# A hybrid encoder block on one core: closing steps of a head group ordered between weight pieces, and q, k, v projections in 512-column products

## The chip, the cores and the metric

The kernel runs on one core of one Trainium2 chip, in one launch. The metric is the device time of a run in microseconds (us). The engines are PE (TensorE: matmuls, and weight loads shown as PEld), DVE (VectorE), ACT (ScalarE), POOL (GpSimd) and SP, which issues the DMA transfers. Each engine works through its own instruction list in order; semaphores hold an instruction until what it needs is there.

## The reference

For one sequence of 256 tokens of width 2048:

```python
h = rms_norm(x, g_mix)
q, k, v, z, f, scal, gates = split(h @ w_in)      # 1024 x5, 32, 4096 columns
y_a = gated_deltanet_branch(q, k, v, z, scal, ...)   # conv, silu, l2 norm, 8 heads of 128,
                                                     # chunks of 64, forward and backward
y_f = real(fft2(f by groups of 128)) @ w_fourier
gate_a, gate_f = split(sigmoid(gates))
x = x + (gate_a * y_a + gate_f * y_f) @ w_o
x = x + square(relu(rms_norm(x, g_mlp) @ w_mlp_up)) @ w_mlp_down
return rms_norm(x, g_final)
```

In the DeltaNet branch each chunk of 64 tokens solves a unit lower triangular system, and chunks are linked by a state per head, in both directions.

## The kernel before

All weights stream once from memory, in pieces of 512 KB (128 x 1024 floats). SP issues the load into a tile `raw` (four buffers). `split` makes two tiles of it (three buffers each): `hi`, a rounded copy on ACT (L88), and `lo`, the remainder, by a subtraction on DVE (L92). The activations are split in the same way, side by side in one tile: `hh[:, k, 0]` is `h_hi`, `hh[:, k, 1]` is `h_lo`. PE sums `hi*hi + hi*lo + lo*hi`. So no weight piece reaches PE before DVE has made its `lo`.

In the order of the streams: k of the first four heads (9 pieces), the other five chunks of q, k, v (40 pieces of `w_qkv`), `w_in` (32 pieces, for z and f), the gates (`w_g`, 64 pieces, eight to a chunk of 512 columns; a gate piece is named here by its number, so the second chunk has pieces 9 to 16), among them and behind them the branches' outputs (`w_dn`, `w_fo`), then `w_o` and the MLP. Two ways of multiplying matter here.

- `pair_fm` (L104 to L130) makes two 128-column blocks of q, k or v, feature-major (features on the partitions), both in one PSUM bank of 512 columns. Per k (16 of them for each block) it issues three products of 256 columns (L121, L122, L127). DVE then multiplies both blocks from PSUM by `rbc`, the rms factor, into `u` (L321). Ten such pairs.
- `stream` (L156) multiplies the other way round: a weight piece of 2 k's by 512 columns is the moving side, and two PSUM banks (token halves) are filled. A gate piece is 12 products of 512 columns (L168 to L170).
- `tile_fm` (L131) exists for the MLP: per k one product of 512 columns (L146), whose moving side is `hi | lo` of the activations, and one of 256 (L149). The two halves of the bank are then added by `add_halves`: a copy on ACT (L153) and an addition on DVE (L154).

The DeltaNet branch works on two groups of four heads, gi = 0 and 1. For a group, DVE inverts small triangles by substitution in 16 steps (L489 `tf`, L491 `Xf`, on a layout made by a round trip through memory: `Mf`). `Xf` goes to memory (`dscr`, L493) and comes back in another layout (`Xh`, eight loads, L498), is copied into `Xc` by ACT (L500) and transposed in blocks by DVE and ACT into `De` and `DT` (L505 to L508). PE joins them into larger inverses (L521, L528, L540, L544). The closing steps of a group follow one from the other: L574 (state, `sF` on DVE L575), L580 (`rS` on DVE L582), L587 (copied by ACT, L588), L593 and L596 (outputs), L601, L604.

The order on every engine is not written by hand: a scheduler with a simulated timeline orders the program's instructions by its own costs and by dependencies. An explicit dependency without a semaphore can be added between two instructions of one engine; it only fixes which comes first.

Of the kernel before, what the change touches and what calls it, by code (L numbers as in the profile page):

```python
# [11 lines left out]
ALU = mybir.AluOpType  # L12
PSUM = bass.MemoryType.PSUM

P = 128
T = 256
# [11 lines left out]
def encoder_block_kernel(ctx, tc, xT, x, g_mix, w_qkv, w_k0, w_in, w_g, w_sc, conv_w, hprm, g_head, w_dn, w_fo, w_o,  # L28
# [16 lines left out]
    def mm_ps():  # L45
        return psm.tile([P, NW], F32, tag="mm", name=nm("mm"))
# [49 lines left out]
    def wtiles(a=KP, n=NW, parts=True):  # L96
        raw = st.tile([P, a, n], F32, tag="raw", bufs=4, name=nm("raw"))
        if not parts:
            return raw, None, None
        hi = st.tile([P, a, n], F32R, tag="hi", bufs=3, name=nm("hi"))  # L100
        lo = st.tile([P, a, n], F32R, tag="lo", bufs=3, name=nm("lo"))
        return raw, hi, lo

    def pair_fm(srcs, ahi, alo):  # L104

        nk = srcs[0].shape[1]
        ps = mm_ps()
        last = None
        for j, src in enumerate(srcs):
            o = ps[:, j * T:j * T + T]  # L110
            for q in range(nk // 8):
                raw, hi, lo = wtiles()
                nc.sync.dma_start(raw.rearrange("p a b -> p (a b)"),
                                  src.rearrange("p k n -> p (k n)")[:, q * 1024:q * 1024 + 1024])
                split(hi, lo, raw)
                hv = hi.rearrange("p a b -> p (a b)")
                lv = lo.rearrange("p a b -> p (a b)")
                for kk in range(8):
                    k = 8 * q + kk
                    cs = slice(kk * P, kk * P + P)  # L120
                    first = pe.matmul(o, hv[:, cs], ahi[:, k, :], start=(k == 0), stop=False)  # L121
                    pe.matmul(o, hv[:, cs], alo[:, k, :], start=False, stop=False)  # L122
                    if last is not None:
                        tc.add_manual_dep(first.ins, last.ins.name, mybir.DependencyInfo(
                            mybir.DependencyClass.NoSync, mybir.DependencyReason.DATA), reason="one group at a time")
                        last = None
                    end = pe.matmul(o, lv[:, cs], ahi[:, k, :], start=False, stop=(k == nk - 1))  # L127
            last = end
        return ps

    def tile_fm(src, ab):  # L131

        ps = mm_ps()
# [18 lines left out]
    def add_halves(dst, ps):  # L152
        act.copy(dst, ps[:, T:2 * T])  # L153
        dve.tensor_tensor(dst, ps[:, 0:T], dst, op=ALU.add)  # L154

    def stream(src, nk, ahi, alo):  # L156

        ps = [mm_ps(), mm_ps()]
        for k0 in range(0, nk, KP):
            raw, hi, lo = wtiles()  # L160
            nc.sync.dma_start(raw, src[:, k0:k0 + KP, :])
            split(hi, lo, raw)
            for kk in range(KP):
                k = k0 + kk
                for tb in range(2):
                    sl = slice(tb * P, tb * P + P)
                    ah, al = ahi[:, k, sl], alo[:, k, sl]
                    pe.matmul(ps[tb], ah, hi[:, kk, :], start=(k == 0), stop=False)  # L168
                    pe.matmul(ps[tb], ah, lo[:, kk, :], start=False, stop=False)  # L169
                    pe.matmul(ps[tb], al, hi[:, kk, :], start=False, stop=(k == nk - 1))  # L170
        return ps


# [133 lines left out]
    def qkv_chunk(c, ps=None):  # L307

        u = pd.tile([P, 4, T + 4], F32, tag="u", bufs=1, name=nm("u"))
        pool.memset(u[:, :, 0:2], 0.0)  # L310
        pool.memset(u[:, :, T + 2:T + 4], 0.0)
        y = pd.tile([P, 4, T], F32, tag="y", bufs=1, name=nm("y"))
        done = 0
        while done < 4:
            if ps is None:
                p = pair_fm([w_qkv[4 * c + done], w_qkv[4 * c + done + 1]], h_hi, h_lo)
                p = p.rearrange("p (a b) -> p a b", a=2)
            else:
                p = ps[done]
            n = p.shape[1]  # L320
            dve.tensor_tensor(u[:, done:done + n, 2:T + 2], p, rbc.unsqueeze(1).to_broadcast([P, n, T]), op=ALU.mult)  # L321
            for j in range(done, done + n):
                cb = 4 * c + j
                act.activation(y[:, j, :], u[:, j, 0:T], AF.Copy, scale=cw[:, cb, 0:1])
                for w in range(1, 5):
                    dve.scalar_tensor_tensor(y[:, j, :], u[:, j, w:w + T], cw[:, cb, w:w + 1], y[:, j, :],
                                             op0=ALU.mult, op1=ALU.add)
            done += n
        return y
# [230 lines left out]
    def dn_out(gi, Kt, offg, offk, rho, Pt, rq, ec):  # L560
        DTv = DT.rearrange("p (d t h) i -> p d t h i", d=2, t=2)
        Y = Kt if gi == 0 else pd.tile([P, 2, 2, 4, P], F32, tag="Kt", name=nm("Y"))
        ohat.append(pd.tile([P, 2, 4, P], F32, tag=f"ohat{gi}", name=nm("ohat")))
        sF = pd.tile([P, 2, 4, P], F32, tag="sF", name=nm("sF"))
        rS = pd.tile([P, 2, 4, P], F32, tag="rS", name=nm("rS"))
        tmp = pd.tile([P, 2, 4, P], F32, tag="tf", name=nm("tmp"))

        def heads_ps():
            return dn_ps().rearrange("p (a b) -> p a b", a=4)

        for d in range(2):
            py = heads_ps()
            for h in range(4):
                pe.matmul(py[:, h], DTv[:, d, d, h], rho[:, d, h], start=True, stop=True)  # L574
            dve.tensor_tensor(sF[:, d], py, ec[:, d].unsqueeze(2).to_broadcast([P, 4, P]), op=ALU.mult)  # L575
            act.copy(Y[:, d, d], py)
        for d in range(2):
            p1 = heads_ps()
            for h in range(4):
                pe.matmul(p1[:, h], offg[d][:, h], sF[:, d, h], start=True, stop=True)  # L580
            for h in range(4):
                dve.scalar_tensor_tensor(rS[:, d, h], p1[:, h], nea[:, 8 * d + 4 * gi + h:8 * d + 4 * gi + h + 1],  # L582
                                         rho[:, 1 - d, h], op0=ALU.mult, op1=ALU.add)
        for d in range(2):
            py = heads_ps()
            for h in range(4):
                pe.matmul(py[:, h], DTv[:, d, 1 - d, h], rS[:, d, h], start=True, stop=True)  # L587
            act.copy(Y[:, d, 1 - d], py)  # L588
        for tb in range(2):
            d = 1 - tb  # L590
            po = heads_ps()
            for h in range(4):
                i1 = pe.matmul(po[:, h], Pt[:, 0, tb, h], Y[:, 0, tb, h], start=True, stop=False)  # L593
                if h:
                    tc.keep_in_program_order(i1)
                i2 = pe.matmul(po[:, h], Pt[:, 1, tb, h], Y[:, 1, tb, h], start=False, stop=True)  # L596
                tc.keep_in_program_order(i2)
            act.activation(tmp[:, d], po, AF.Copy, scale=-1.0)
            p2 = heads_ps()
            for h in range(4):  # L600
                pe.matmul(p2[:, h], offk[:, 1 - tb, h], sF[:, d, h], start=True, stop=True)  # L601
            oh = ohat[gi][:, tb]
            for h in range(4):
                dve.scalar_tensor_tensor(oh[:, h], p2[:, h], eab[:, 8 * d + 4 * gi + h:8 * d + 4 * gi + h + 1],  # L604
                                         tmp[:, d, h], op0=ALU.mult, op1=ALU.add)

            ov = pd.tile([P, 4], F32, tag="ov", bufs=2, name=nm("ov"))
            for h in range(4):
                act.activation(tmp[:, d, h], oh[:, h], AF.Square, accum_out=ov[:, h:h + 1])
            rqt = rq[:, 4 * tb:4 * tb + 4]  # L610
            r2 = pd.tile([P, 4], F32, tag="r2", bufs=2, name=nm("r2"))
            pool.tensor_tensor(r2, rqt, rqt, op=ALU.mult)
            pool.tensor_tensor(ov, ov, r2, op=ALU.mult)
            pool.tensor_scalar(ov, ov, 1.0 / P, EPS, op0=ALU.mult, op1=ALU.add)
            pool.tensor_tensor(ov, ov, neg_half[:, 0:4], op=ALU.pow)
            pool.tensor_tensor(fsc[:, gi, tb], ov, rqt, op=ALU.mult)
# [34 lines left out]
    def gates(dst, c):  # L651

        ps = stream(w_g[c], KD, h_hi, h_lo)
        for tb in range(2):
            act.activation(dst[tb], ps[tb], AF.Tanh, scale=rstdh[:, tb:tb + 1])  # L655
# [3 lines left out]
    def m_cols(c):  # L659
        return [merged[:, tb, c * NW:c * NW + NW] for tb in range(2)]  # L660

    for c in range(4):
        gates(m_cols(c), c)


    o_hi = pd.tile([P, NH, T], F32R, tag="Kt", name="o_hi")
# [312 lines left out]
```

## Time and profile before

| | |
|---|---|
| median of 3 runs | 1390.75 us (1389.53 to 1393.6) |
| profiled execution | 1391.09 us, span 1389.3 us |
| mean granted clock of PE | 0.997 |
| PE busy | 1373.4 us (99%) |
| DVE busy | 864.2 us (62%) |
| ACT busy | 688.5 us (50%) |
| loads of weights | 250 MB of 255.6 MB, mean 184 GB/s |

A row of a group gives busy time and mean ns of one instruction, then the idle time of the engine before them and what ended it. A row of the timeline starts with the start in us and the duration. A matmul's duration includes its way through the array, so the pace of PE is read from starts, not from durations. Idle time of an engine that is not the bound costs nothing.

### The profile page before, as it was taken

Reading aid. Unit: us, or ns where it says so; the run is one execution under the profiler, and the core shown is the slowest. Engines: PE = TensorE matmul, PEld = TensorE weight load, DVE = VectorE, ACT = ScalarE, POOL = GpSimd, SP = SyncE. Lnnn points to the kernel's source line nnn. Section 1 sums busy time; section 2 is a strip of 40 time slices with the busy share of each in tenths; the row PEclk is TensorE's granted clock in tenths of the full one; section 3 lists DMA queues with packets and bytes.
Section 4 is the critical chain, followed back from the end, with each engine's and each line's share of the span. In section 5 each row is a group of like instructions: output and inputs, shape, how many; then the busy total and the mean of one; then the engine's idle time right before and its main releaser. Section 6 shows DMA issues by size and latency. Waiting matters only on the chain.

```text
span 1389.3 us, 19766 instructions
## 1 busy us (share of the span) xinstructions
PE 1373.4 (99%) x7646; PEld 1188.0 (86%) x7646; DVE 864.2 (62%) x1233; ACT 688.5 (50%) x1038; POOL 36.0 (3%) x60
## 2 busy tenths in 40 slices
PE   9999999999999999999999999999999999999997
PEld 8999997888888888888888888888888888888886
DVE  7869997855556555655666666444456666645553
ACT  6586746454444444455554454333345445434443
POOL 2001010100000000000000000000000000000000
PEclk9999999999999999999999999999999999999999
DMA  8456455354566556676565556666665555666663
GB/s 288 148 168 184 152 166 176 93 166 137 176 201 181 156 177 188 194 269 186 175 200 185 193 193 188 193 190 195 195 196 183 192 190 192 185 197 193 190 197 132
DMA packets 88399, 255.61 MB, mean 184 GB/s; under 512 B 25456, under 2 KB 25456, under 8 KB 87920
## 3 DMA queue, kind: packets, MB, share of 16 engines
q1 hardware_dynamic: 87312, 250.15, 58.8%
q10 hardware_dynamic: 992, 4.19, 0.8%
q8 instruction: 60, 0.98, 0.3%
q14 instruction: 35, 0.29, 0.1%
HBM read 251.16 MB, written 3.15 MB: 183 GB/s over the span
## 4 chain that ended last, share of the span: by engine, by line
PE 94%; issue 1%; DVE 1%; DMA 1%; ACT 1%; SPq 1%; POOLq 0%; POOL 0%; DVEq 0%; ACTq 0%
PE mm L146 17%; PE mm L170 10%; PE mm L169 10%; PE mm L168 10%; PE mm L149 9%; PE mm L831 7%; PE mm L829 7%; PE mm L830 7%; PE mm L122 3%; PE mm L121 3%; PE mm L127 3%; PE mm L866 1%; PE mm L864 1%; PE mm L865 1%; DVE lo L92 0%
## 5 line engine op out<-in xcount | busy, mean ns | idle before, releaser
L92 DVE TENSOR_TENSOR lo<-raw,hi 128x1024 fp32r<-128x1024 f32 (+1 forms) x459 | 560.8, 1222 | 339.4 <-ACT hi L88 330.7
L88 ACT ACTIVATE hi<-raw 128x1024 fp32r<-128x1024 f32 (+1 forms) x459 | 485.9, 1059 | 422.6 <-PE mm L831 181.7
L146 PE MATMUL mm<-hh,hi 128*128 128x512 f32 x1024 | 245.1, 391 | 0.0
L146 PEld LDWEIGHTS mm<-hh,hi 128*128 128x128 f32 x1024 | 188.2, 188 | 36.2
L831 PE MATMUL mm<-hi,rl 128*128 128x512 f32 x448 | 174.6, 390 | 0.0
L830 PE MATMUL mm<-lo,rh 128*128 128x512 f32 x448 | 174.5, 389 | 0.0
L829 PE MATMUL mm<-hi,rh 128*128 128x512 f32 x448 | 156.2, 390 | 0.0
L169 PE MATMUL mm<-lo,hh 128*128 128x512 f32 x384 | 151.4, 394 | 0.0
L170 PE MATMUL mm<-hi,hh 128*128 128x512 f32 x384 | 150.8, 393 | 0.0
L168 PE MATMUL mm<-hi,hh 128*128 128x512 f32 x384 | 142.4, 392 | 0.4 <-ACT merged L655 0.4
L149 PEld LDWEIGHTS mm<-hh,lo 128*128 128x128 f32 x1024 | 131.5, 191 | 5.1
L149 PE MATMUL mm<-hh,lo 128*128 128x256 f32 x1024 | 133.2, 283 | 0.0
L153 ACT COPY rt<-mm 128x256 f32<-128x256 f32 x64 | 23.8, 372 | 164.5 <-PE mm L146 164.5
L831 PEld LDWEIGHTS mm<-hi,rl 128*128 128x128 f32 x448 | 84.2, 188 | 17.5
L830 PEld LDWEIGHTS mm<-lo,rh 128*128 128x128 f32 x448 | 84.1, 188 | 17.5
L829 PEld LDWEIGHTS mm<-hi,rh 128*128 128x128 f32 x448 | 84.1, 188 | 17.3
L154 DVE TENSOR_TENSOR rt<-mm,rt 128x256 f32<-128x256 f32 x64 | 27.2, 424 | 110.5 <-ACT rt L153 110.5
L122 PE MATMUL mm<-hh,hi 128*128 128x256 f32 x320 | 90.8, 284 | 0.0
L121 PE MATMUL mm<-hh,hi 128*128 128x256 f32 x320 | 90.7, 284 | 0.0
L127 PE MATMUL mm<-hh,lo 128*128 128x256 f32 x320 | 90.5, 284 | 0.0
L168 PEld LDWEIGHTS mm<-hi,hh 128*128 128x128 f32 x384 | 71.9, 188 | 15.2 <-ACT merged L655 0.6
L169 PEld LDWEIGHTS mm<-lo,hh 128*128 128x128 f32 x384 | 72.5, 189 | 14.2
(309 smaller groups left out, 1690.4 us busy)
## 6 DMA issues: line engine op xcount, KB each, us to landing
raw<-in_w_up_dram SPq DMA_DIRECT2D x128, 512.0 KB, 3.9
raw<-in_w_down_dram SPq DMA_DIRECT2D x128, 512.0 KB, 3.5
raw<-in_w_g_dram SPq DMA_DIRECT2D x64, 512.0 KB, 3.8
raw<-in_w_qkv_dram SPq DMA_DIRECT2D x40, 512.0 KB, 4.2
raw<-in_w_in_dram SPq DMA_DIRECT2D x32, 512.0 KB, 3.9
raw<-in_w_o_dram SPq DMA_DIRECT2D x32, 512.0 KB, 4.4
raw<-in_w_dn_dram SPq DMA_DIRECT2D x16, 512.0 KB, 3.6
raw<-in_w_fo_dram SPq DMA_DIRECT2D x16, 512.0 KB, 3.6
```

The source lines that it names most:

```text
L88: act.activation(hi, src, AF.Copy, scale=scale)
L92: dve.tensor_tensor(lo, src2, hi.bitcast(F32), op=ALU.subtract)
L121: first = pe.matmul(o, hv[:, cs], ahi[:, k, :], start=(k == 0), stop=False)
L122: pe.matmul(o, hv[:, cs], alo[:, k, :], start=False, stop=False)
L146: pe.matmul(ps, hv[:, cs], ab[:, k].rearrange("p a b -> p (a b)"), start=(k == 0), stop=(k == KD - 1))
L149: pe.matmul(ps[:, 0:T], lv[:, cs], ab[:, k, 0], start=False, stop=False)
L168: pe.matmul(ps[tb], ah, hi[:, kk, :], start=(k == 0), stop=False)
L169: pe.matmul(ps[tb], ah, lo[:, kk, :], start=False, stop=False)
L170: pe.matmul(ps[tb], al, hi[:, kk, :], start=False, stop=(k == nk - 1))
L829: pe.matmul(ps[tb], ah, hi[:, kk, :], start=(k == 0), stop=False)
L830: pe.matmul(ps[tb], ah, lo[:, kk, :], start=False, stop=False)
L831: pe.matmul(ps[tb], al_, hi[:, kk, :], start=False, stop=(k == 31))
```

## The change

`pair_fm` is gone; each q, k, v block is a `tile_fm` in a bank of its own, followed by a copy on ACT and an addition on DVE, and for each pair of blocks one multiplication by `rbc` from SBUF. `stream` notes the last product of each piece in `ends`. The closing steps of group 0 note six first products in `steps` (two of L580, two of L587, two of L593). After the second gate chunk is written, `spread(0)` orders step i behind the last product of piece i of that chunk.

```diff
-    def pair_fm(srcs, ahi, alo):
...
+    ends = []
+    steps = []
+
+    def spread(s0):
+
+        for step, end in zip(steps[s0:], ends):
+            tc.add_manual_dep(step.ins, end.ins.name, mybir.DependencyInfo(
+                mybir.DependencyClass.NoSync, mybir.DependencyReason.DATA), reason="weights between the steps")
...
     def stream(src, nk, ahi, alo):
 
         ps = [mm_ps(), mm_ps()]
+        ends.clear()
...
-                    pe.matmul(ps[tb], al, hi[:, kk, :], start=False, stop=(k == nk - 1))
+                    end = pe.matmul(ps[tb], al, hi[:, kk, :], start=False, stop=(k == nk - 1))
+            ends.append(end)
...
-                p = pair_fm([w_qkv[4 * c + done], w_qkv[4 * c + done + 1]], h_hi, h_lo)
-                p = p.rearrange("p (a b) -> p a b", a=2)
+                n = 2
+                for j in range(done, done + n):
+                    p = tile_fm(w_qkv[4 * c + j], hh)
+                    uj = u[:, j, 2:T + 2]
+                    act.copy(uj, p[:, T:2 * T])
+                    dve.tensor_tensor(uj, p[:, 0:T], uj, op=ALU.add)
+                un = u[:, done:done + n, 2:T + 2]
+                dve.tensor_tensor(un, un, rbc.unsqueeze(1).to_broadcast([P, n, T]), op=ALU.mult)
...
-                pe.matmul(p1[:, h], offg[d][:, h], sF[:, d, h], start=True, stop=True)
+                i1 = pe.matmul(p1[:, h], offg[d][:, h], sF[:, d, h], start=True, stop=True)
+                if gi == 0 and h == 0:
+                    steps.append(i1)
...
     for c in range(4):
         gates(m_cols(c), c)
+        if c == 1:
+            spread(0)
```

The scheduler makes a new order from it. On PE, at the closing steps of group 0, before: the steps stand in one piece (numbers behind names tell tiles apart; `rho`, `sF`, `rS` are the chunk states of the group, `off` its link matrices).

```order
L170 MATMUL mm_3358<-hi_3486,hh 128x512
L574 MATMUL dn_1728<-rho_1214,DT 128x128 x4
L580 MATMUL dn_1735<-sF_1718,off_666 128x128 x4
L580 MATMUL dn_1744<-sF_1718,off_666 128x128 x4
L587 MATMUL dn_1753<-rS_1719,DT 128x128 x4
L587 MATMUL dn_1759<-rS_1719,DT 128x128 x4
L593 MATMUL dn_1765<-grp_528 128x128
```

After, on PE, the second of the L580 steps (now L571) and the first of the L587 steps (now L580), with `hi_3274` of gate piece 11 and `hi_3292` of piece 12:

```order
L571 MATMUL dn_1636<-sF_1610,off_666 128x128 x4
L151 MATMUL mm_3236<-hi_3274,hh 128x512
L152 MATMUL mm_3236<-lo_3275,hh 128x512
L153 MATMUL mm_3236<-hi_3274,hh 128x512
L151 MATMUL mm_3236<-hi_3274,hh 128x512
L152 MATMUL mm_3236<-lo_3275,hh 128x512
L153 MATMUL mm_3236<-hi_3274,hh 128x512
L151 MATMUL mm_3235<-hi_3292,hh 128x512
L151 MATMUL mm_3236<-hi_3292,hh 128x512
L580 MATMUL dn_1645<-rS_1611,DT 128x128 x4
L152 MATMUL mm_3235<-lo_3293,hh 128x512
```

The steps now have weight products of half a piece or more between them; pieces 9, 10 and 11 are used half by half around them.

On DVE, at the end of the second group's inverse, before (`lo_3563` and `lo_3581` are the remainders of gate pieces 12 and 13):

```order
L491 TENSOR_TENSOR Xf_2248<-Xf_2248,tf_2249 128x16
L646 SCALAR_TENSOR_TENSOR zs_3055<-tz_3202,zs_3055 128x512
L673 SCALAR_TENSOR_TENSOR ohat_1717<-ohat_1717,fsc,zs_1227 128x128 x4
L646 SCALAR_TENSOR_TENSOR zs_3055<-tz_3206,zs_3055 128x512
L555 TENSOR_TENSOR E_1825<-E_1825,aux_3229 128x4x128
L555 TENSOR_TENSOR E_1825<-E_1825,aux_3238 128x4x128
L92 TENSOR_TENSOR lo_3563<-raw_3561,hi_3562 128x1024
L92 TENSOR_TENSOR lo_3581<-raw_3579,hi_3580 128x1024
L505 STREAM_TRANSPOSE De<-Xc_2333 32x8x32
```

After, the same place on DVE (`lo_3293` is the remainder of gate piece 12):

```order
L480 TENSOR_TENSOR tf_2087<-Mf_2085,Xf_2086 128x16
L482 TENSOR_TENSOR Xf_2086<-Xf_2086,tf_2087 128x16
L643 SCALAR_TENSOR_TENSOR zs_2785<-tz_2932,zs_2785 128x512
L643 SCALAR_TENSOR_TENSOR zs_2785<-tz_2936,zs_2785 128x512
L496 STREAM_TRANSPOSE De<-Xc_2171 32x8x32 x4
L575 SCALAR_TENSOR_TENSOR rS_1611<-dn_1627,nea,rho_1160 128x128 x4
L92 TENSOR_TENSOR lo_3293<-raw_3291,hi_3292 128x1024
```

Between `Xf` and `De` stood two `lo`, two `E` and one `ohat`; now only the two `zs` stand there, and `lo` of piece 12 comes behind `De`. The `lo` of piece 11 stands thirty steps of the inverse ahead of these rows.

On DVE, behind the end of the first group's inverse (`De<-Xc_803` is the first group's) the rows are now:

```order
L482 TENSOR_TENSOR Xf_718<-Xf_718,tf_719 128x16
L92 TENSOR_TENSOR lo_2862<-raw_2860,hi_2861 128x1024
L92 TENSOR_TENSOR lo_2880<-raw_2878,hi_2879 128x1024
L409 TENSOR_TENSOR rho_2528<-aux_2529,nk_2017 128x512
L92 TENSOR_TENSOR lo_2898<-raw_2896,hi_2897 128x1024
L409 TENSOR_TENSOR rho_2528<-aux_2535,nk_2017 128x512
L317 SCALAR_TENSOR_TENSOR y_2544<-u_2541,cw,y_2544 128x256 x4
L496 STREAM_TRANSPOSE De<-Xc_803 32x8x32
```

Before, there were three `lo`, one `rho` and sixteen `y` (convolution taps, L326) between the same two.

On ACT, the rows ahead of `hi` of gate piece 12 are now:

```order
L642 ACTIVATE zs_2785<-mm_2787,rstd 128x512
L491 COPY Xc_2171<-Xh_2162 128x16x2x16
L497 COPY De<-Xc_2171 32x8x32 x4
L88 ACTIVATE hi_3292<-raw_3291 128x1024
L88 ACTIVATE hi_3310<-raw_3309 128x1024
```

Before, `hi` of pieces 12 and 13 stood ahead of the copy into `Xc`.

More of the change, by code (lines that the diff above doesn't have):

```diff
@@ L102, in wtiles @@
         return raw, hi, lo
-    def pair_fm(srcs, ahi, alo):
[L106 to L129, printed above, removed]
     def tile_fm(src, ab):
@@ L315, in qkv_chunk @@
             if ps is None:
-                p = pair_fm([w_qkv[4 * c + done], w_qkv[4 * c + done + 1]], h_hi, h_lo)
-                p = p.rearrange("p (a b) -> p a b", a=2)
+                n = 2
[6 more added lines that the diff above has]
+                dve.tensor_tensor(un, un, rbc.unsqueeze(1).to_broadcast([P, n, T]), op=ALU.mult)
             else:
                 p = ps[done]
-            n = p.shape[1]
-            dve.tensor_tensor(u[:, done:done + n, 2:T + 2], p, rbc.unsqueeze(1).to_broadcast([P, n, T]), op=ALU.mult)
+                n = p.shape[1]
+                dve.tensor_tensor(u[:, done:done + n, 2:T + 2], p, rbc.unsqueeze(1).to_broadcast([P, n, T]),
+                                  op=ALU.mult)
             for j in range(done, done + n):
@@ L586, in dn_out @@
             for h in range(4):
-                pe.matmul(py[:, h], DTv[:, d, 1 - d, h], rS[:, d, h], start=True, stop=True)
+                i1 = pe.matmul(py[:, h], DTv[:, d, 1 - d, h], rS[:, d, h], start=True, stop=True)
+                if gi == 0 and h == 0:
+                    steps.append(i1)
             act.copy(Y[:, d, 1 - d], py)
@@ L595, in dn_out @@
                     tc.keep_in_program_order(i1)
+                elif gi == 0:
+                    steps.append(i1)
                 i2 = pe.matmul(po[:, h], Pt[:, 1, tb, h], Y[:, 1, tb, h], start=False, stop=True)
```

## The prediction

> **What bounds the kernel now.** I read the page first (shares, chain by line, costly groups), then the waits of PE, then the chain of waits and the timeline between 195 and 290 us, and last the busy time by stretches.
>
> ```profile
> span 1389.3 us, 19766 instructions
> PE 1373.4 (99%) x7646; PEld 1188.0 (86%) x7646; DVE 864.2 (62%) x1233; ACT 688.5 (50%) x1038; POOL 36.0 (3%) x60
> ...
> PE 94%; issue 1%; DVE 1%; DMA 1%; ACT 1%; SPq 1%; POOLq 0%; POOL 0%; DVEq 0%; ACTq 0%
> ```
>
> PE is busy for 99% of the span and is 94% of the chain that ends last, so what an edit saves on PE counts in full, and so does every microsecond for which PE is made to wait. The shares hide where DVE is full. The next view is the busy time by stretches (length, PE with its count, PE's weight loads, DVE, ACT, POOL, granted clock, DMA share, GB/s):
>
> ```profile
> 60.00:110.00 50.00, 50.00 (x327) 45.81 (x327) 38.33 (x72) 35.50 (x72) 7.49 (x6) 1.00 0.53 169
> 110.00:210.00 100.00, 100.00 (x761) 96.45 (x761) 95.42 (x191) 61.60 (x133) 9.70 (x13) 1.00 0.57 168
> ```
>
> Between 110 and 210 us, where two thirds of the q, k, v blocks run beside the preparation of the DeltaNet chunks, DVE works 95.4 of 100 us. PE is the bound there only by a hair, since each weight piece needs its `lo` from DVE.
>
> PE's few named stalls stand after that stretch, in the waits of PE and its timeline, and behind one of them the granted clock is 0.76:
>
> ```profile
> PE dn L540 <- DVE DT L532: 1.9, 1, 1.9
> PE dn L528 <- ACT W L524: 0.8, 1, 0.8
> ...
> 231.00:238.00 7.00, 7.00 (x38) 6.07 (x37) 5.93 (x16) 3.01 (x5) 0.00 (x0) 0.76 0.58 199
> ...
> 251.67 1.05 PE L574 MATMUL dn<-rho,DT 128*128 128x128 f32 x8
> 252.56 1.06 PE L580 MATMUL dn<-sF,off 128*128 128x128 f32 x8
> ...
> 264.83 0.50 PE L168 MATMUL mm<-hi,hh 128*128 128x512 f32 x1 [0.37 <-ACT merged L655]
> ```
>
> **Part 1, the projections.** Per k a block gave three 256-column products and now gives one 512-column and one 256-column product. PE's chain and timeline price both forms by their starts:
>
> ```profile
> 33.38 0.28 PE L121 MATMUL mm<-hh,hi 128*128 128x256 f32 x1
> ...
> 35.90 0.28 PE L121 MATMUL mm<-hh,hi 128*128 128x256 f32 x1
> ...
> 696.94 3.65 PE mm L146 x16
> 700.60 1.91 PE mm L149 x16
> ```
>
> Twenty-one products lie between the first two rows, 2.52 us, so 0.120 us each and 0.360 us per k. In the other form, which `tile_fm` already has elsewhere, a k takes 3.65/16 + 1.91/16 = 0.228 + 0.119 = 0.347 us. That is 0.011 to 0.013 us per k (0.120 is rounded), times 320 k's 3.5 to 4 us; I take **-3.6 us**, 0.18 us per block.
>
> The Trainium skill, "TensorE: Matmul & The Clock Gate", section "Back-to-back issue gap", gives an isolated gap of N/2.4 + 2.5 ns: 109 ns for 256 columns and 216 ns for 512. An estimate from that page is 3 x 109.2 - (215.8 + 109.2) = 2.6 ns per k, or 0.8 us in all; by it the sum below would be 2.8 us higher. The gaps of this trace are longer by a twentieth for 512 columns and a tenth for 256, and the measured rows decide.
>
> The halves must now be added: per block a copy on ACT and an addition on DVE, of a kind that exists already.
>
> ```profile
> L153 ACT COPY rt<-mm 128x256 f32<-128x256 f32 x64 | 23.8, 372 | 164.5 <-PE mm L146 164.5
> L154 DVE TENSOR_TENSOR rt<-mm,rt 128x256 f32<-128x256 f32 x64 | 27.2, 424 | 110.5 <-ACT rt L153 110.5
> ```
>
> ACT gets 20 x 0.372 = 7.4 us, which its idle 38 of 100 us hide; if that cover were gone, `hi` would be late by as much. DVE gets 20 x 0.424 = 8.5 us, and the ten multiplications by `rbc` stay at their price (the nearest 128x512 groups read from SBUF or PSUM alike near 0.69 us). By counts of L121 in stretches 196 of the 320 k's lie between 110 and 210 us:
>
> ```profile
> 0.00:60.00 60.00, 17.04 (x60) 11.50 (x60) 1.00 0.68 222
> 60.00:110.00 50.00, 18.24 (x65) 12.33 (x65) 1.00 0.53 169
> 110.00:210.00 100.00, 55.41 (x196) 37.55 (x196) 1.00 0.57 168
> ```
>
> So 12.25 blocks fall there: PE's own work shrinks by 12.25 x 0.18 = 2.2 us, DVE's grows by 12.25 x 0.424 = 5.2 us to 100.6. DVE's waits in that stretch were few:
>
> ```profile
> DVE u L321 <- PE mm L127: 1.2, 3, 0.7
> DVE lo L92 <- ACT hi L88: 1.2, 4, 0.5
> DVE tf L489 <- DMA Mf<-dscr: 0.7, 1, 0.7
> DVE rho L418 <- PE aux L417: 0.5, 1, 0.5
> ```
>
> If these 3.6 us stay, DVE needs 104.2. DVE takes over as the bound: the stretch ends 0.6 to 4.2 us later and not 2.2 earlier. The other 7.75 blocks bring their -1.4 us, beside a DVE with 12 of 50 us idle.
>
> **Part 2, a round trip with less cover at the end of that stretch.** `Xf` of one group goes to memory and comes back before DVE can go on with `De`:
>
> ```profile
> 199.48 0.17 DVE L491 TENSOR_TENSOR Xf<-Xf,tf 128x16 f32<-128x16 f32 x1
> ...
> 204.07 1.67 DVE L326 SCALAR_TENSOR_TENSOR y<-u,cw,y 128x256 f32<-128x256 f32 x4
> ...
> 210.75 0.43 DVE L505 STREAM_TRANSPOSE De<-Xc 32x256 f32<-32x256 f32 x1 [0.76 <-ACT Xc L500]
> ```
>
> It takes 11.1 us (199.65 to 210.75), of which DVE idles 0.76. In the new order only two `lo`, two `rho`, one more `lo` and four `y` stand between, 3 x 1.22 + 2 x 0.69 + 4 x 0.42 = 6.7 us against 10.3 of before, so DVE's wait grows by about 3.2 us (10.3 counts the gaps). With Part 1 DVE is 3.8 to 7.4 us late when it turns to the gate pieces. I take **+5 us** for the stretch in place of -2.2; both ends stay.
>
> **Part 3, the closing steps.** Before, the first group's closing steps run from 252.56 to 264.83 us with no weight product between: 12.27 us for 80 products of 128 columns, which at (252.56 - 251.67)/8 = 0.111 us are 8.9. The 3.4 us left are waits for DVE and ACT; with weight pieces between the steps they should go: **-3.4 us**. What is late next is the group's `merged` part, which nobody on PE needs soon.
>
> As pieces move, PE's L540 product now has two more weight pieces ahead of it, so its 1.9 us should go too, and with it the low clock: 0.24 of the 7 us from 231 to 238 is 1.7 us. With L528's 0.8 that is **-4.4 us**. If the cover fails, they return in full.
>
> **Part 4, the price of the moved steps.** The second group's inverse on DVE (`tf`, `Xf`) and its `De` used to lie around the first group's steps. Its round trip before, on DVE, SP and ACT:
>
> ```profile
> 266.97 0.17 DVE L491 TENSOR_TENSOR Xf<-Xf,tf 128x16 f32<-128x16 f32 x1
> 267.23 0.33 SPq L493 DMA_DIRECT2D dscr<-Xf  x1
> 269.60 4.92 SPq L498 DMA_DIRECT2D Xh<-dscr  x8
> ...
> 273.44 2.45 DVE L92 TENSOR_TENSOR lo<-raw,hi 128x1024 fp32r<-128x1024 f32 x2 [0.80 <-ACT hi L88]
> 276.52 0.67 ACT L500 COPY Xc<-Xh 128x512 f32<-128x512 f32 x1 [1.88 <-DMA Xh<-dscr]
> 277.22 0.43 DVE L505 STREAM_TRANSPOSE De<-Xc 32x256 f32<-32x256 f32 x1 [1.32 <-ACT Xc L500]
> ```
>
> Xf ends at 267.14 and De starts at 277.22, 10.1 us; DVE fills that with other work, two `lo` among it. In the new order DVE runs `sF`, `lo` of piece 11, thirty `tf`/`Xf`, two `zs`, then `De`, an `rS`, and only then `lo` of piece 12. ACT has the copy into `Xc` and the `De` copies ahead of `hi` of piece 12 as well. Behind the waiting `De` are queued all later `lo`, and PE waits for those. Durations of the groups:
>
> ```profile
> L491 DVE TENSOR_TENSOR Xf<-Xf,tf 128x126 f32<-128x126 f32 (+22 forms) x62 | 16.4, 264 | 1.0
> L489 DVE TENSOR_TENSOR tf<-Mf,Xf 128x126 f32<-128x126 f32 (+22 forms) x62 | 16.2, 261 | 3.7 <-DMA Mf<-dscr 2.5
> L582 DVE SCALAR_TENSOR_TENSOR rS<-dn,nea,rho 128x128 f32<-128x128 f32 x16 | 4.5, 343 | 0.0
> L575 DVE TENSOR_TENSOR sF<-dn,ec 128x512 f32<-128x512 f32 x4 | 2.8, 690 | 0.6 <-PE dn L574 0.4
> L418 DVE TENSOR_TENSOR rho<-aux,nk 128x512 f32<-128x512 f32 x4 | 2.8, 688 | 0.7 <-PE aux L417 0.7
> ```
>
> Count both engines from the end of the product that `sF` waits for. DVE: `sF` 0.7, `lo` of piece 11 1.2, thirty steps of the inverse at 0.263 = 7.9, the round trip 10.1, four `De` at 0.43 = 1.7, `rS` 1.0 (the four took 1.04 us in the chain of before; 0.343 each, overlapping), `lo` of piece 12 1.2: 23.8 us. PE: six products each of six half pieces, 36 x 0.228 = 8.2, eight closing products 0.9, two `hi` products of piece 12 and four closing ones 0.9: 10.0 us. PE stands still for **13.8 us**. The least is 12, if the thirty steps and the trip each lose a tenth; the most 15, with the 11.1 us of the first group's trip. `sF` ties `lo` of piece 11 to PE, so DVE cannot have run ahead.
>
> A stop of that length should lower the clock: the nearest row is the 1.9 us before L540, which cost 1.7 us. I add **+1.7 us** (nothing to 3.4). The same page of the Trainium skill, section "Part 1: The HAM clock gate", puts the drop after an idle window of about 3.4 us and as much busy time before full speed; here the drop followed 1.9 us of idle time, and no run here shows a longer one in the body of the kernel.
>
> **The sum.** -1.4 (blocks outside the full stretch) + 5 - 3.4 - 4.4 + 13.8 + 1.7 = +11.3 us on the profiled 1391.1 us (span 1389.3 and 1.8 around it), 1402.4. The median of the runs is 0.3 us lower, so 1402. A real difference is one above 0.3%, 4.2 us (1386.6 to 1394.9).
>
> **The rivals.**
>
> *The trip is short or covered, and the change is faster.* The one mechanism is whether DVE stands at `De`. Without any standing there DVE still needs 23.8 - 10.1 = 13.7 us against PE's 10.0, a stall of 3.7 us and no low clock; with spare time on DVE in Part 1 as well, the sum is -1.4 - 2.2 - 3.4 - 4.4 + 3.7 = -7.7, or 1383. It is no longer faster from a sum of -4.2 on, that is a stall of 7.2 us, or 3.5 us of standing at `De`. Against it stand both measured trips, 10.1 and 11.1 us, and only two `zs` (0.69 each) that DVE can do meanwhile. For it: the first group's trip cost DVE only 0.76 us. Chance 0.10.
>
> *The losses and gains cancel.* DVE's 5.2 us in Part 1 fit into gaps that the page's sums don't show (-2.2 in place of +5), and Part 4 costs its least, 12 us, without a clock drop: -1.4 - 2.2 - 3.4 - 4.4 + 12 = +0.6, or 1392. For it: PE's busy 100 of 100 us says only that `lo` was never late by much, not how early it was. Chance 0.18.
>
> *More low clocks.* If waits of 2 to 4 us in Part 2 and at the end of the second group each bring 1.7 us, as the 1.9 us at L540 did, and L540's own comes back with 3.6, three such give +5.1 and the time is 1407 to 1411. The 0.8 us at L528 brought none, so the length decides. By the page's 3.4 us window they would bring nothing, and the sum stays at 1402. Chance 0.19.
>
> My forecast (1397 to 1406) has 0.53. Slower takes 0.53 + 0.19 and 0.01 of the cancelling case, faster the first rival and 0.01 of it, the same the rest: 0.73, 0.11 and 0.16. The range runs from 1391 (the least of Parts 1 and 4) to 1411.
>
> **What the profile after would show.** Products of `tile_fm` in pairs of 0.228 and 0.119 us; DVE over 98% busy between 110 and 210 us; 30 `tf`/`Xf` in one block behind `lo` of gate piece 11 and then an idle time of 8 us and more of DVE at `De<-Xc`, released by ACT's `Xc`; PE waiting for `lo` in the second gate chunk by 10 us or more, with a clock below 0.9 behind it; no wait at L540's counterpart and none between the closing steps. If the wait at `De` is under 4 us, Part 4 is wrong; if DVE stays under 97% and no `lo` is late before the gate pieces, Part 1 is.

## The result, and the profile after

The changed kernel takes 1401.28 us (median of 6 runs, 1400.12 to 1401.73); before takes 1389.87 us beside it (median of 6). The ratio is 1.0072, with a 95% interval of 1.0061 to 1.0083, so it is slower by about 11 us. The prediction said 1402.

The page and the busy time by stretches of the changed kernel:

```profile
span 1400.0 us, 19163 instructions
PE 1372.4 (98%) x7326; PEld 1171.8 (84%) x7326; DVE 871.1 (62%) x1253; ACT 695.2 (50%) x1058; POOL 39.4 (3%) x60
...
PE 94%; DVE 3%; issue 1%; DMA 1%; ACT 1%; SPq 0%; POOLq 0%; POOL 0%; ACTq 0%; DVEq 0%
...
110.00:210.00 100.00, 97.85 (x564) 85.78 (x563) 94.42 (x190) 64.27 (x145) 16.64 (x15) 1.00 0.55 163
211.00:222.00 11.00, 7.99 (x113) 5.39 (x113) 10.86 (x22) 9.94 (x20) 0.00 (x0) 0.84 0.51 164
252.00:270.00 18.00, 7.12 (x27) 5.65 (x26) 11.44 (x37) 3.60 (x5) 0.00 (x0) 0.72 0.37 85
```

PE's work is a little less, and the span is 10.7 us more. PE now stands in two places. One is 211 to 222 us, the start of the gate pieces. The other is 252 to 270 us, where PE is busy for only 7 of 18 us and the granted clock is 0.72. The waits of PE name what ended the stops:

```profile
PE mm L151 <- ACT zs L642: 10.9, 1, 10.9
PE mm L151 <- ACT hi L88: 2.8, 2, 2.1
PE mm L151 <- DVE u L305: 1.6, 1, 1.6
```

The long one is not where Part 4 of the prediction put it. The timelines of PE, ACT and DVE around it:

```profile
251.87 1.05 PE L565 MATMUL dn<-rho,DT 128*128 128x128 f32 x8
263.80 0.79 PE L151 MATMUL mm<-hi,hh 128*128 128x512 f32 x1 [10.88 <-ACT zs L642]
...
267.81 0.63 PE L151 MATMUL mm<-hi,hh 128*128 128x512 f32 x1
268.24 0.48 PE L152 MATMUL mm<-lo,hh 128*128 128x512 f32 x1
...
263.06 0.69 ACT L642 ACTIVATE zs<-mm,rstd 128x512 f32<-128x512 f32 x1 [8.80 <-DVE tf L480]
...
252.96 0.69 DVE L566 TENSOR_TENSOR sF<-dn,ec 128x512 f32<-128x512 f32 x1
...
254.69 0.29 DVE L480 TENSOR_TENSOR tf<-Mf,Xf 128x135 f32<-128x135 f32 x1
...
262.85 0.18 DVE L480 TENSOR_TENSOR tf<-Mf,Xf 128x16 f32<-128x16 f32 x1
...
272.40 1.79 DVE L496 STREAM_TRANSPOSE De<-Xc 32x256 f32<-32x256 f32 x4 [5.90 <-ACT Xc L491]
...
275.24 1.22 DVE L92 TENSOR_TENSOR lo<-raw,hi 128x1024 fp32r<-128x1024 f32 x1
```

PE stands ahead of the first product of gate piece 9, and not of piece 12. That product opens a new PSUM bank, and the bank it was given still holds a z product. ACT empties it by writing `zs1` (L642). But `zs1` lies in the memory of `Mf`, the input of the second group's inverse: `Mf = pd.tile(..., tag=("sF", "zs1")[gi])`. So ACT waits until the last `tf` has read `Mf`, at 263.03, and PE goes on when the first `zs` is done.

The pool of these PSUM banks has four (`bufs=4`). Ahead of piece 9 two hold the z products and two the products of the first gate chunk. In the kernel before, ACT emptied one of the latter in time: it ran the gate's `merged` ahead of `zs`, and piece 9 got its bank from that, with a wait of 0.37 us. ACT's row in the kernel before:

```profile
264.10 1.26 ACT L655 ACTIVATE merged<-mm,rstdh 128x512 f32<-128x512 f32 x2
```

In the changed kernel ACT writes the first `merged` only at 294.76 us. `merged` lies in the memory of `grp0` (both have `tag="merged"`), which the last closing steps of group 0 read (`dn<-grp`), and `spread` puts these steps behind pieces 9 to 14. So in this order the first chunk's banks come free only behind those pieces, and piece 9 is left with a z product's.

DVE does stand at `De`, 5.9 us (Part 4 of the prediction expected 8 us and more); at 276 us PE uses piece 12 without a wait, because PE itself is late by then.

### The profile page after: what moved, and what is told of

It is laid out like the page before. It is cut to its first block, busy times and chain, and to the rows that moved or that the text cites. A ratio compares the mean times of both kernels' runs of the same rounds, so it can differ in the third digit from the quotient of the medians.

```text
span 1400.0 us, 19163 instructions
## 1 busy us (share of the span) xinstructions
PE 1372.4 (98%) x7326; PEld 1171.8 (84%) x7326; DVE 871.1 (62%) x1253; ACT 695.2 (50%) x1058; POOL 39.4 (3%) x60
## 4 chain that ended last, share of the span: by engine, by line
PE 94%; DVE 3%; issue 1%; DMA 1%; ACT 1%; SPq 0%; POOLq 0%; POOL 0%; ACTq 0%; DVEq 0%
PE mm L119 22%; PE mm L122 11%; PE mm L152 10%; PE mm L153 10%; PE mm L151 10%; PE mm L828 7%; PE mm L830 7%; PE mm L829 7%; PE mm L865 1%; PE mm L863 1%; PE mm L864 1%; DVE lo L92 1%; DVE tf L480 1%; DMA raw<-in_w_k_dram 0%; DVE Xf L482 0%
## 5 line engine op out<-in xcount | busy, mean ns | idle before, releaser
L119 PE MATMUL mm<-hh,hi 128*128 128x512 f32 x1344 | 322.4, 391 | 0.0
L119 PEld LDWEIGHTS mm<-hh,hi 128*128 128x128 f32 x1344 | 246.7, 188 | 47.6
L122 PEld LDWEIGHTS mm<-hh,lo 128*128 128x128 f32 x1344 | 174.7, 191 | 7.2
L122 PE MATMUL mm<-hh,lo 128*128 128x256 f32 x1344 | 178.5, 283 | 0.0
L151 PE MATMUL mm<-hi,hh 128*128 128x512 f32 x384 | 144.7, 397 | 15.3 <-ACT zs L642 10.9
L153 PE MATMUL mm<-hi,hh 128*128 128x512 f32 x384 | 151.6, 395 | 0.0
L126 ACT COPY rt<-mm 128x256 f32<-128x256 f32 x64 | 23.8, 372 | 164.8 <-PE mm L119 164.8
L151 PEld LDWEIGHTS mm<-hi,hh 128*128 128x128 f32 x384 | 72.8, 190 | 31.0 <-ACT zs L642 11.1
L153 PEld LDWEIGHTS mm<-hi,hh 128*128 128x128 f32 x384 | 73.0, 190 | 14.5
L152 PE MATMUL mm<-lo,m_hi 128*128 128x512 f32 x128 | 49.9, 390 | 0.0
L153 PE MATMUL mm<-hi,m_lo 128*128 128x512 f32 x128 | 49.8, 389 | 0.0
```

Source lines behind the costliest of these rows:

```text
L119: pe.matmul(ps, hv[:, cs], ab[:, k].rearrange("p a b -> p (a b)"), start=(k == 0), stop=(k == KD - 1))
L122: pe.matmul(ps[:, 0:T], lv[:, cs], ab[:, k, 0], start=False, stop=False)
L153: end = pe.matmul(ps[tb], al, hi[:, kk, :], start=False, stop=(k == nk - 1))
```

## The experiments

Each is compared with the kernel before, run beside it on the same chip (medians of before 1390.1 to 1390.5 us).

**e3: another place for zs1.**

```diff
-        zs.append(pd.tile([P, 2, NW], F32, tag=f"zs{c}", name=nm("zs")))
+        zs.append(pd.tile([P, 2, NW], F32, tag=("zs0", "u")[c], name=nm("zs")))
```

> The changed kernel with one buffer moved: the second z tile (zs1) lies in the memory of u, which is free by then, and no longer in that of Mf, which the second group's inverse reads to its last step. Theory of the bank (PE's 10.9 us stop ahead of gate piece 9 comes from a z product's PSUM bank that ACT cannot empty while Mf is in use; the clock behind it costs 2 us): the stop goes, 1387 to 1390 us. The scheduler now also puts De of the second group behind lo of piece 13. Rival (the stop is the round trip's, only shown at another place): some 10 us of stop remain, 1398 to 1402. Rival (the slowness comes from the projections' additions): no change, 1401.

It took 1390.62 us, ratio 1.0004 (0.9994 to 1.0014). The stretch that was empty is full, at full clock:

```profile
252.00:270.00 18.00, 18.00 (x100) 15.55 (x100) 15.87 (x43) 7.41 (x9) 0.00 (x0) 1.00 0.50 148
```

All 11 us come back. In this kernel the order has changed too (`De` behind `lo` of piece 13), so e3 removes the bank's wait and DVE's standing ahead of piece 12 together. The next two take them apart.

**e4: only De and Xc moved back behind pieces 12 and 13.** `xc` and `de` are the copy into `Xc` and the first `De` of group 1; `trip` holds these two, `parts_` holds `hi` and `lo` of each piece of the second gate chunk.

```diff
             spread(0)
+            for late, early in zip(trip, parts_[4]):
+                tc.add_manual_dep(late.ins, early.ins.name, ...)
```

> The changed kernel with De and the Xc copy of the second group ordered behind lo and hi of gate piece 13; everything else around it keeps its order, and zs1 still shares Mf's memory. The prediction's Part 4 (lo of piece 12 late behind the round trip is what stops PE): 12 to 15 us come back, 1387 to 1390. Theory of the bank: the stop ahead of piece 9 stays at 10 to 11 us and DVE's standing was covered by it: 1400 to 1402.

It took 1401.39 us, ratio 1.0084 (1.0069 to 1.0099): nothing came back. PE's waits still have the whole stop:

```profile
PE mm L158 <- ACT zs L652: 10.9, 1, 10.9
```

So the round trip is not what stopped PE in the changed kernel.

**e7: the bank free, the trip kept ahead of piece 12.** As e3, with the reverse order of e4 (`hi` and `lo` of piece 12 behind `Xc` and the last `De`; `trip` holds those two of group 1).

```diff
+            for early, late in zip(trip, parts_[3]):
+                tc.add_manual_dep(late.ins, early.ins.name, ...)
```

> As e3 (zs1 in the memory of u), but hi and lo of gate piece 12 are ordered behind the Xc copy and the last De of the second group. It lays the cost that Part 4 worked out open by itself: by Part 4 PE stops 13 to 15 us at piece 12 and loses about 2 us of clock, 1401 to 1406; if the round trip is covered at that place anyway, it is as e3, 1387 to 1390.

It took 1405.95 us, ratio 1.0118 (1.0103 to 1.0133), 15.3 us above e3. PE's and DVE's timeline, and the stretch:

```profile
277.87 1.22 PE L158 MATMUL mm<-hi,hh 128*128 128x512 f32 x2 [13.43 <-ACT hi L93]
280.00 0.79 PE L159 MATMUL mm<-lo,hh 128*128 128x512 f32 x1 [0.91 <-DVE lo L97]
...
276.90 1.78 DVE L504 STREAM_TRANSPOSE De<-Xc 32x256 f32<-32x256 f32 x4 [9.14 <-ACT Xc L499]
...
262.00:286.00 24.00, 9.66 (x36) 7.52 (x35) 10.38 (x31) 7.86 (x15) 0.00 (x0) 0.64 0.35 87
```

Laid open, the wait that Part 4 worked out costs 13.4 + 0.9 = 14.3 us of standing, first for `hi` of piece 12 (on ACT behind the copy into `Xc`), then for its `lo`; 13.8 were forecast, and low clock comes on top. The two waits lie over each other: with the bank held, the trip costs nothing; with the bank free and the order kept, it costs more than the bank did.

**e2: the ordering of the closing steps alone**, with `pair_fm` as before.

> The ordering of the closing steps alone, with the projections as before (256-column products in pairs). If the ordering carries the slowdown by way of the z product's PSUM bank: a stop of about 11 us ahead of gate piece 9 and 2 us of low clock, less the 3.4 us between the closing steps: 1398 to 1402. Rival: the stop needs the later DVE of the projections as well: 1386 to 1390.

It took 1398.33 us, ratio 1.0057 (1.0042 to 1.0073). The stop is there without the new projections, 9.2 us long:

```profile
PE mm L178 <- ACT zs L666: 9.2, 1, 9.2
```

**e1: the projections alone**, without the call of `spread`.

> The projections' part alone, without the ordering of the closing steps (which stand again in one piece). By Part 1 and 2 of the prediction the additions on a full DVE eat up what PE saves: -1.4 + 5 on the time before, less up to 3.6 of L540's wait, so 1388 to 1394. Rival: the saving is kept, 1386. Rival: the projections carry the whole slowdown, 1399 or more.

It took 1390.26 us, ratio 1.0000 (0.9991 to 1.0010). Piece 9 gets its bank from `merged` again, with a wait of 0.4 us. The saving on PE is there and is lost again. PE's timeline of e1:

```profile
187.50 0.47 PE L151 MATMUL mm<-hi,hh 128*128 128x512 f32 x1 [1.65 <-DVE u L305]
198.36 0.50 PE L152 MATMUL mm<-lo,hh 128*128 128x512 f32 x1 [0.54 <-DVE lo L92]
211.26 0.73 PE L151 MATMUL mm<-hi,hh 128*128 128x512 f32 x2 [1.27 <-ACT hi L88]
...
215.09 1.22 PE L151 MATMUL mm<-hi,hh 128*128 128x512 f32 x2 [2.07 <-ACT hi L88]
```

The first two stops come from the additions (a bank that DVE had not read yet, a `lo` behind them), the last two from the first group's round trip: `hi` stands on ACT behind the copy into `Xc`, which waits for the load.

**e6: without the additions on DVE** (`dve.tensor_tensor(uj, p[:, 0:T], uj, op=ALU.add)` taken out of the changed kernel).

> The changed kernel without the twenty additions of the halves on DVE (it leaves the hi*hi + lo*hi half out of q, k and v; the copies on ACT stay). Part 1 priced them at 3 to 6 us of PE's time by way of a full DVE: then 1396 to 1398. Part 2's own round trip of the first group (3.5 us of standing at De, low clock behind it) and the bank's stop stay. Rival: the additions lie beside other work: 1400 to 1402.

It took 1402.33 us, ratio 1.0083 (1.0069 to 1.0097), no faster than the changed kernel. The stops of 1.6 and 0.5 us are gone, PE is busy 100 of 100 us there, and the time comes back behind it, at the first group's inverse:

```profile
110.00:210.00 100.00, 100.00 (x575) 87.94 (x574) 92.25 (x183) 65.73 (x147) 16.37 (x14) 1.00 0.55 165
...
PE mm L151 <- ACT zs L641: 11.2, 1, 11.2
PE mm L151 <- ACT hi L88: 2.4, 1, 2.4
PE dn L518 <- ACT W L514: 2.3, 1, 2.3
```

So the additions, some 8.5 us of DVE by the prediction's count, are not what sets the time of the changed kernel. But the bank's stop stays in e6, and DVE's inverse sets its end (263.97 us, in the changed kernel 263.80), so what PE wins ahead of it need not show; e6 with `zs1` moved was not run. The order behind the additions differs a little, too (nine `y` and no longer four ahead of the first `De`), so this test leaves the share of the additions in the trip's start open.

**e12: the first group's trip taken away.** As e3; `Xh` of the first group is loaded from the inverse's input, and `De` is held at its place behind the same `lo`.

```diff
-        back = dxo.rearrange(...)
+        back = (dscr[0][0] if gi == 0 else dxo).rearrange(...)
```

> As e3 (the changed kernel, zs1 in the memory of u), but the first group's Xh is loaded from the array that holds the inverse's input, written long before, so its De no longer waits for the trip of Xf (the first group's blocks of the inverse are left out by this); De stands on DVE where it stood, behind the same lo. If the trip of Part 2 eats the projections' saving: the stops at the first gate pieces (2.1 and 0.9 us) and the low clock behind (2.3) go, 1384 to 1387 against e3's 1390.6. If the additions on a full DVE eat it: 1389 to 1391.

It took 1388.01 us, ratio 0.9983 (0.9973 to 0.9992), 2.6 us under e3, less than expected. The stretch of the first gate pieces in e12, and then in e3:

```profile
211.00:222.00 11.00, 10.85 (x162) 8.36 (x161) 10.88 (x20) 7.00 (x12) 0.00 (x0) 1.00 0.63 125
```

```profile
211.00:222.00 11.00, 7.99 (x90) 5.29 (x91) 10.61 (x22) 9.37 (x20) 0.00 (x0) 0.69 0.49 160
```

The 3 us of standing and the low clock (0.69 to 1.00) are gone as expected. Part of it comes back elsewhere, the wait for `u` at 185 us growing from 1.6 to 2.6 us and one for `o_hi` at 345 us from 0.5 to 1.8, with a granted clock of 0.72 over 346 to 352 us behind it:

```profile
PE mm L158 <- DVE u L313: 2.6, 1, 2.6
PE mm L158 <- ACT o_hi L93: 1.8, 1, 1.8
```

**e11: De of the first group behind gate piece 1** (as e3, with an ordering like that of e4 for group 0).

> As e3 (the changed kernel, zs1 in the memory of u), and the first group's De and Xc copy are ordered behind lo and hi of gate piece 1. By Part 2 DVE's 3.5 us of standing at the first De then costs PE nothing: the stop of 2.1 us, the 0.9 ahead of it and some 2.3 us of low clock go, 1385 to 1388. Rival: the stop only moves to the next piece, 1389 to 1391.

It took 1395.11 us, ratio 1.0034 (1.0021 to 1.0046): slower than e3 by 4.5 us, and slower than both the expectation and its rival had it. The stop at the first gate pieces is down to 0.7 us, and the steps behind `De` are late instead, in both groups:

```profile
PE dn L522 <- ACT tmp L605: 4.5, 1, 4.5
PE dn L541 <- DVE DT L533: 3.0, 1, 3.0
```

**e8: ordering with the old projections and zs1 moved.**

> The ordering of the closing steps with the projections as before, and zs1 in the memory of u. Without the bank's stop the ordering should bring its gain, the 3.4 us between closing steps: 1385 to 1388, below e3's 1390.6, because the projections' saving is lost to DVE there. Rival: the projections bring their 3.6 us, and this is 1392 to 1395.

It took 1392.14 us, ratio 1.0014 (1.0006 to 1.0023). The closing steps' gain is spent at the second group's first product with `De`:

```profile
286.70 1.06 PE L536 MATMUL dn<-De,Kt 32*32 32x32 f32 x32 [3.77 <-ACT tmp L619]
```

In e3 the same wait is 1.4 us. The expectation was wrong, and the time is the rival's: 1.5 us above e3, which suggests that part of the projections' saving is left in e3.

**e9 and e10: zs1 moved, and no explicit ordering**, with the old projections (e9) and the new ones (e10).

> The kernel before with zs1 in the memory of u and nothing else. The scheduler spreads the closing steps by itself. From e8 (1392.1, with the ordering): 1390 to 1393, since the 3.4 us won at the closing steps come back as the 3.8 us stop at the second group's De. Rival: the closing steps' gain stays, 1386 to 1388.

> The projections' part with zs1 in the memory of u, and no ordering of the closing steps. With the bank free the scheduler puts weight pieces between the steps by itself, nearly as in e3. So as e3: 1389.5 to 1391.5. If the explicit ordering does anything of its own then: 1392 or more.

e9 took 1392.99 us, ratio 1.0019 (1.0010 to 1.0029); e10 took 1391.08, ratio 1.0005 (0.9995 to 1.0014). With the bank free the scheduler spreads the closing steps by itself, and the explicit ordering changes nothing that can be told: e10 is within 0.5 us of e3, e9 within 0.9 of e8.

**e13: a shorter trip?** As e3, with half of the `Xh` loads issued by POOL.

```diff
-                nc.sync.dma_start(Xh[...], back[half, b])
+                (nc.sync, nc.gpsimd)[half].dma_start(Xh[...], back[half, b])
```

> As e3 (the changed kernel, zs1 in the memory of u), with four of the eight Xh loads of each group issued by POOL and no longer all by SP (eight issues took SP 4.0 us). The scheduler also puts De of the first group behind one more lo and four more y. If the eight issues are what makes the trip long and DVE's standing at De is what stops PE: the trip is 1 to 2 us shorter, the stop of 2.1 us and its low clock go, 1386 to 1388. If POOL's issues are slow, or as in e11 the later De only moves the stop: 1390 to 1396.

It took 1394.52 us, ratio 1.0029 (1.0019 to 1.0039). The trip is no shorter (`Xf` ends at 200.46 and `De` starts at 211.84, 11.4 us), although SP's issues took half as long. PE's stop at the first gate pieces stays (2.2 us), and a new one stands at 284.77 us, ahead of a gate product whose bank comes free with `merged`; ACT runs that behind the second group's `Xc`, and the granted clock is 0.50 over 284 to 290 us:

```profile
PE mm L151 <- ACT merged L652: 3.4, 1, 3.4
```

No version faster than both kernels came of this; e12 is faster only by leaving a step out.

## Why the prediction was right, point by point

- **The time and the direction** were right, 1402 against 1401.3, and the closeness is in part luck: a stop of another origin stood in for the forecast one, and errors inside cancel. Of the 10.7 us between the two profiled spans 1.7 arise in the first 17 us, ahead of the first changed product (33.8 us): the same product starts at 15.50 us before and at 17.20 after, at a granted clock of 1.00 and 0.76 over 10.0 to 17.2 us. The traces of e3, e7 and e11 have this low clock at the start too, the others do not, so single traces compare only to about 2 us. From there to the last eight products of L574 (now L565) the changed kernel is 1.5 us faster, and starts them at 251.87 us against 251.67; the forecast for this stretch was -1.4 + 5 - 4.4 = -0.8. What is left of the loss comes behind it: 10.9 of stop and 2.2 of low clock, less the 3.4 between the closing steps.
- **Part 4, the failed step, with a sentence of Part 3.** "PE stands still for 13.8 us" ahead of piece 12 because `lo` stands behind `De`: that wait is real in e7 (14.3 us), but in the changed kernel PE stood ahead of piece 9 for 10.9 us, held by a PSUM bank. DVE's side of the count came out: from `sF` at 252.96 to the end of `lo` of piece 12 at 276.46 are 23.5 us, 23.8 forecast. PE's side failed, 10.0 us of products up to piece 12, since PE could not open piece 9. Part 3 put this wait at nothing: the `merged` part would be late, "which nobody on PE needs soon", but piece 9 needs the bank that `merged` empties. I read the order of DVE and SP and did not follow PSUM and memory that tiles share: which reader frees the bank that a product opens, and what that reader waits for. The size came out near by luck, because both waits contain the same thirty steps of the inverse: the bank's ends with them, at 263, and De's one trip later. That the steps' cover fails was right; what it fails on was not.
- **Its low clock**, 1.7 us forecast: the ten products from 263.80 to 268.24 took 4.44 us where 10 x 0.228 is 2.28: 2.2 us.
- **Part 1**: the 3.6 us of PE's saving fit e1, which has L540's stop no longer either (3.6 us with its clock) and pays for both with 5.5 us of stops and the clock behind them. "DVE over 98% busy between 110 and 210 us" was wrong: 94.4, less than before. DVE did not become the bound of the whole stretch; the additions cost two short stops, 1.65 and 0.50 us in the changed kernel, where 2.8 to 6.4 were forecast (0.6 to 4.2 later, not 2.2 earlier), and in e6 the time is the same without them.
- **Part 2**: the wait at the first `De` was to grow from 0.76 by 3.2 us and is 3.52. Its price was 3.2; PE waits 0.71 and 2.08 us there, and the clock of 0.84 over 11 us is 1.8 more, 4.6 in all. So Part 1 was sized too high and Part 2 too low. Their sum, a loss of 7.2 us (5 in place of -2.2), was 2.2 + 4.6 = 6.8. These rows of the changed kernel show it:

```profile
188.74 0.47 PE L151 MATMUL mm<-hi,hh 128*128 128x512 f32 x1 [1.65 <-DVE u L305]
...
215.74 0.73 PE L151 MATMUL mm<-hi,hh 128*128 128x512 f32 x2 [2.08 <-ACT hi L88]
...
210.94 0.43 DVE L496 STREAM_TRANSPOSE De<-Xc 32x256 f32<-32x256 f32 x1 [3.52 <-ACT Xc L491]
```

- **Part 3**: no wait for `DT` or `rS` is left on PE in the changed kernel, so the waits between the closing steps and L540's stop went, as forecast. In e3, where no bank hides it, that leaves the time equal to before: the gains pay for Part 1 and 2 and no more.
- **The rival of more low clocks** says that the length of a stop decides; that was wrong. The clock fell after a stop of 1.55 us at the start of the changed kernel, and stayed at 1.00 after 2.59 us in e12 and 2.19 us in e13.
- **What stays open**: how much of the late `Xf` of the first group comes from the additions, and whether a loss at 340 us in e12 is due to the missing trip or to its order.

## What to carry to other kernels

A step that is ordered later holds everything that shares its resources, and an order on the engines does not show that: ask of each moved instruction which PSUM bank and which reused tile it opens, who empties that, and which tile that reader writes into. A stop removed may only uncover another beneath it, as the bank and the trip here: cure one alone and look, in both orders. A long chain (here 9 to 12 us through memory) can take back what is saved on the engine that waits for it.

## What the runs showed of the hardware

The granted clock fell after stops of 1.55 us (changed kernel, 0.57 over 12 to 16 us), 1.89 us (kernel before, 0.76 over 231 to 238 us), 2.08 us (changed kernel, 0.84 over 211 to 222 us) and 10.88 us (0.72 over 252 to 270 us). After the last one PE's products ran at half pace for about 4.4 us. It stayed at 1.00 after a stop of 1.65 us (changed kernel, 188 to 210 us), after 2.19 us (e13, 215 to 240 us) and after 2.59 us (e12, 188 to 210 us). So the length of one stop does not settle in these runs whether the clock falls; what else does was not tested.

The Trainium skill ("TensorE: Matmul & The Clock Gate", section "Part 1: The HAM clock gate") puts the drop after an idle window of about 3.4 us. Here it came after single stops shorter than that, and the half pace after the long stop lasted longer.
